# GpSimd adds weight blocks, and a third pair of k tiles takes seven block products for eight, in an encoder's second FFN product

## The chip, the cores and the metric

The kernel runs on one core of a Trainium2 chip. The metric is the device time of one execution in microseconds (us). The engines are TensorE (PE: matmuls; PEld: its weight loads), VectorE (DVE), ScalarE (ACT), GpSimd (POOL) and SyncE (SP, which issues nearly all loads).

## What is computed

Two layers of an encoder over 256 tokens with a width of 2048. Each layer mixes the tokens in three ways (an mLSTM, latent attention, dilated attention), projects the result and ends with a feed-forward part, the stage of this change:

```
h = rms_norm(x, norm_ff)
u = relu(h @ w_ff1)            # 256 x 8192
x = x + (u * u) @ w_ff2        # 8192 -> 2048
```

All is float32. The kernel gets float32 accuracy from a faster matmul type by splitting each operand into a high half (`hi`, rounded) and a low half (`lo`, what the rounding left), so that every block product is three matmuls: hi by hi, hi by lo, lo by hi.

## The kernel before, in words

**Stages.** Each layer runs through the mixers, the output projection, and then four chunks of 2048 of the 8192 FFN columns. A chunk has a first product (16 tiles `u` of 128 columns, 32 weight units) and a second product, in which the 16 tiles are multiplied by their 2048 rows of `w_ff2`. "kp" counts pairs of neighbouring k tiles, 0 to 7.

**The second product.** The output has 2048 columns: four units of 512, taken two at a time (`fast_groups`, line 1272): a left unit g and a right unit g+1, each with two PSUM banks, one for each 128 tokens. A plain step (`token_group`, line 469) takes one weight unit, 128 x 1024 values (two k tiles of 512 columns), and makes 2 k tiles x 2 token tiles x 3 = 12 matmuls of 512 columns. For the kp in `FAST` (line 307), (2, 5), left and right are done together: 2 token tiles x 2 k tiles times 2 k tiles x 2 units is a 2 x 2 product of blocks, and it takes seven block products (21 matmuls) where plain steps take eight (24). For that it needs sums of blocks of both sides. The activations' sums (`act_sums`, line 1253) are made once a chunk. The weights' sums are four adds of 128 x 512 for each such pair, made on DVE, in `Weights.split`, as the first part of a unit of kind "sums". So a pair has four weight units: "first" and "second" (the loaded blocks of the left and the right unit; of the second only half is used), "sums" and "more sums" (two added blocks each). Four more PSUM banks hold products that several sums share; `fast_end` (line 1320) adds them to x, `ff2_end` (line 1368) adds the left and right banks. The order of a group is: left 0, left 1, pair 2, left 3, left 4, pair 5, left 6, left 7, then the six right steps. The last chunk of layer 0 has no pairs.

**Weights.** `Weights` (line 222) walks one list of units for the whole kernel. SP loads a unit into one of three buffers (`wst`); ACT casts it to `hi`; DVE subtracts to get `lo`. Four hi/lo buffers (`B_HL`, line 1397), so units are split up to three ahead of PE. A load is issued for each split unit that was a loaded one. The added blocks lie in `ws`, two tiles of the pool `big` (four tiles), beside the split activation sums `s_hl`.

**Order.** Each engine works through its instructions in program order. That order is written by a planner (`Stream`, line 123): small generators, the tasks, are stepped when their due time has come on a clock that counts the cost of the matmuls, from a table of costs per engine.

**The start.** `warm_up` (line 553) runs `WARM` = 10 products of 128 columns while the first loads are on their way.

The functions that the change touches:

Of the kernel before, what the change touches and what calls it, by code (L numbers as in the profile page):

```python
# [17 lines left out]
P = 128  # L18
# [50 lines left out]
MLA_AT = ((3, 2), (3, 3), (3, 7), (4, 3), (5, 0), (6, 1))  # L69
MARGIN = 0.3  # L70
ML_AT_ONCE = 2
WARM = 10

# [135 lines left out]
def tile2k(c, name, dtype=F32R):  # L209
    return c.t2.tile([P, 512], dtype, tag="t2", name=name)  # L210
# [11 lines left out]
class Weights:  # L222
# [3 lines left out]
    def __init__(self, c, items):  # L226
        self.c, self.items = c, items
        self.srcs = [(i, src, n) for i, (src, n, kind) in enumerate(items) if src is not None]
        self.st, self.hl = {}, {}
        self.i = self.d = self.k = 0  # L230

    def load(self):
        c = self.c
        if self.d == len(self.srcs):
            return
        i, src, n = self.srcs[self.d]
        self.st[i] = c.wp.tile([P, 1024], F32, tag="wst", name="wst", bufs=c.B_ST)
        for cols in self.pieces(i):
            c.nc.sync.dma_start(self.st[i][:, cols], src[:, cols])
        self.d += 1  # L240

    def pieces(self, i):
# [4 lines left out]
    def split(self):  # L247

        c, nc, k = self.c, self.c.nc, self.k
        src, n, kind = self.items[k]  # L250
        hi = c.wp.tile([P, 1024], F32R, tag="whi", name="whi", bufs=c.B_HL)
        lo = c.wp.tile([P, 1024], F32R, tag="wlo", name="wlo", bufs=c.B_HL)
        if kind == "sums":
            a, b = self.st.pop(k - 2), self.st.pop(k - 1)

            x, y = (c.big.tile([P, 1040], F32, tag="big", name="ws") for _ in range(2))
            self.st[k + 1] = y
            pieces, st = [slice(0, 512), slice(512, 1024)], x
        else:
            st = self.st[k] if kind else self.st.pop(k)  # L260
            if kind == "second":
                st = st[:, 512:]
                pieces = [slice(0, 512)]
            elif kind == "more sums":
                st = self.st.pop(k)
                pieces = [slice(0, 512), slice(512, 1024)]
            else:
                pieces = self.pieces(k)

        def parts():  # L270
            if kind == "sums":
# [5 lines left out]
            for cols in pieces:  # L277
                nc.scalar.copy(hi[:, cols], st[:, cols])
            yield
            for cols in pieces:  # L280
                nc.vector.tensor_tensor(out=lo[:, cols], in0=st[:, cols], in1=hi[:, cols].bitcast(F32),
                                        op=ALU.subtract)

        t = c.s.spawn(parts())
        if kind != "more sums":
            c.s.step(t)
        else:
            t.due = max(t.due, self.sums.due)
        if kind == "sums":
            self.sums = t  # L290
        self.hl[k] = (hi, lo, t)
        self.k += 1

    def next(self):
        while self.k < min(len(self.items), self.i + self.c.B_HL - 1):
            loads = self.items[self.k][0] is not None
            self.split()
            if loads:
                self.load()
# [14 lines left out]
def weight_order(c, depth):  # L314
    srcs = []
    for l in range(depth):
# [8 lines left out]
        for ch in range(NCHUNK):  # L325
            srcs += [(c.w_ff1[l, ch * KT + i, half], 1024) for i in range(KT) for half in range(2)]
            if not fast(l, ch, depth):
                srcs += [(c.w_ff2[l, ch, g, kp], 1024) for g in range(NX) for kp in range(KT // 2)]
                continue
            for g in range(0, NX, 2):  # L330
                for kp in range(KT // 2):
                    if kp in FAST:
                        srcs += [(c.w_ff2[l, ch, g, kp], 1024, "first"), (c.w_ff2[l, ch, g + 1, kp], 1024, "second"),
                                 (None, 1024, "sums"), (None, 1024, "more sums")]
                    else:
                        srcs.append((c.w_ff2[l, ch, g, kp], 1024))
                srcs += [(c.w_ff2[l, ch, g + 1, kp], 1024) for kp in range(KT // 2) if kp not in FAST]
    return [(*a, None)[:3] for a in srcs]
# [325 lines left out]
def k_rope(c, z1):  # L664
# [17 lines left out]

    kh = c.cp.tile([P, S], F32R, tag="krh", name="krh", bufs=1)
    kl = c.cp.tile([P, S], F32R, tag="krl", name="krl", bufs=1)
    nc.scalar.activation(kl[MLA_ROPE:], c.const[MLA_ROPE:, :S], AF.Copy, scale=0.0)
# [205 lines left out]
def ml_gates(c, z1):  # L891
# [59 lines left out]

    ahl = c.cp.tile([P, 2, S], F32R, tag="ml_ahl", name="ml_ahl", bufs=1)
    A2 = A.unsqueeze(1).to_broadcast([64, 2, S])
# [170 lines left out]
def mixers(c, prepare, after):  # L1124
    nc, s = c.nc, c.s
    dv = c.cp.tile([P, 2, NT, DIL_H * DIL_DH], F32R, tag="dv", name="dv", bufs=1)
    c.dv = {(i, tt): dv[:, i, tt] for i in range(2) for tt in range(NT)}
# [95 lines left out]
def ffn(c, l, last_layer, depth):  # L1223
# [4 lines left out]
    for ch in range(NCHUNK):  # L1228
        us = [None] * KT
        quick = fast(l, ch, depth)  # L1230
        uf = {kp: tile2k(c, "uf", F32) for kp in FAST} if quick else {}
        sums = {}
        for f in range(KT):
            ps = c.gps.tile([P, 512], F32, tag="g", name="g")
            for half in range(2):
                w_half(c, c.xg, 8 * half, ps, half == 0, half == 1)
            kp, i = divmod(f, 2)
            c.s.spawn(ff1_end(c, ps, f, us, uf[kp][:, i * S:(i + 1) * S] if kp in uf else None))
            if i and kp in uf:
                c.s.spawn(act_sums(c, us, kp, uf[kp], sums))  # L1240
        for g in range(0, NX, 2):
# [10 lines left out]

def act_sums(c, us, kp, u, sums):

# [9 lines left out]
    yield  # L1264
    hl = c.big.tile([P, 1040], F32R, tag="big", name="s_hl")
    nc.scalar.copy(hl[:, :512], sf)
# [5 lines left out]
def fast_groups(c, us, sums, l, ch, g, last, last_layer, nxt):  # L1272
# [11 lines left out]
    left, right = two_banks(c), None  # L1284
    banks = None
    for kp in range(KT // 2):
        if kp not in FAST:
            token_group(c, us, left, 512, [kp])
            continue
        first, end = kp == FAST[0], kp == FAST[-1]  # L1290
        if first:
            right = two_banks(c)
            c.s.until(lambda: c.s.room["m"] >= 4)
            c.s.give(m=-4)
            banks = [new_bank(c, "fast") for _ in range(4)]
        p1, q5, p6, p7 = banks
        c.s.until(lambda: kp in sums)
        s1, s2, s3, s4 = sums[kp]
        w = c.w.next()
        product(p1, u(2 * kp, 0), w, one, first, end)  # L1300
        product(left[0], u(2 * kp + 1, 0), w, two, False, False)
        w = c.w.next()
        product(right[0], s4, w, one, first, False)
        w = c.w.next()
        product(q5, s1, w, one, first, end)
        product(p6, s2, w, two, first, end)
        w = c.w.next()
        product(p7, s3, w, one, first, end)
        product(left[1], u(2 * kp + 1, 1), w, two, False, False)
        if end:  # L1310
            done = c.s.spawn(fast_end(c, banks, g))
    c.s.spawn(ff2_end(c, left, g, l, ch, last_layer, nxt, done))
    kps = [kp for kp in range(KT // 2) if kp not in FAST]
    token_group(c, us, right, 512, kps[:-1] if last else kps, opened=(0,))
    if last:
        last_unit(c, us, right, 512)
    c.s.spawn(ff2_end(c, right, g + 1, l, ch, last_layer, nxt, done))
# [70 lines left out]
def encoder(ctx, tc, xT, x, const, vecs, w_in, w_in1, w_mla, w_out, w_ff1, w_ff2, out):  # L1388
# [30 lines left out]
    c.xts = xts = []  # L1419
    c.mean = c.cp.tile([P, 16], F32, tag="mean", name="mean")[:, :2]  # L1420
    nc.vector.memset(c.mean, 1.0 / D)
# [164 lines left out]
```

## Time and profile before

| | us |
|---|---|
| median of 3 runs | 2108.2 (2107.16 to 2109.35) |
| profiled execution, its own time | 2108.59 |
| its span, first to last instruction | 2106.8 |
| PE busy in the span | 2094.5 |
| DVE busy | 1582.6 |
| ACT busy | 1125.8 |
| POOL busy | 13.8 |

The granted clock of TensorE is 0.999 of full speed over the span. How to read it: busy times are unions over the span, PE's ends are modelled and its matmuls overlap, so the duration shown for one matmul (0.39 us) is longer than the distance to the next. A releaser behind an idle time (`<-`) is what ended it. L104 and L200 are the lines of the helpers that record all DVE, ACT and POOL instructions and all matmuls; so instructions are told apart by their tiles.

### The profile page before, as it was taken

To read this page: it belongs to the slowest core of one execution; us is meant where nothing else is said; L and a number is where in the kernel's file an instruction comes from. 1 tells how busy PE (TensorE), PEld (TensorE's weight loads), DVE (VectorE), ACT (ScalarE), POOL (GpSimd) and SP (SyncE) were. 2 spreads that over 40 slices of the span, in tenths; PEclk is the share of its full clock that TensorE was granted. 3 is DMA by queue.
4 is the path that set the end of the run, shared out by engine and by line. 5 is a ranking of instruction groups with operands and counts; after the bars stand their busy time and mean duration, and the time that the engine had idled before them with its cause. 6 is when DMAs were issued, how large, how long until landed. Compare 5 with 4: busy or idle time off the path is not lost.

```text
span 2106.8 us, 29301 instructions
## 1 busy us (share of the span) xinstructions
PE 2094.5 (99%) x10792; PEld 1791.9 (85%) x10792; DVE 1582.6 (75%) x2624; ACT 1125.8 (53%) x1870; POOL 13.8 (1%) x35
## 2 busy tenths in 40 slices
PE   9999999999999999999999999999999999999999
PEld 8888888888888888888888888888888888888887
DVE  6789865788778778775557888567877787787786
ACT  5777654454455444544456675554544454454453
POOL 1000000000000000001000000000000000000000
PEclk9999999999999999999999999999999999999999
DMA  7544455666656665656555445556665566666665
GB/s 264 162 169 156 150 170 181 194 189 204 191 182 200 200 191 183 210 192 200 181 170 166 140 137 165 175 180 193 190 203 191 178 206 199 189 191 201 190 193 176
DMA packets 109151, 389.91 MB, mean 185 GB/s; under 512 B 12368, under 2 KB 12496, under 8 KB 108752
## 3 DMA queue, kind: packets, MB, share of 16 engines
q1 hardware_dynamic: 107136, 384.71, 57.8%
q10 hardware_dynamic: 1872, 3.33, 0.4%
q8 instruction: 84, 1.38, 0.3%
q14 instruction: 59, 0.48, 0.1%
HBM read 385.90 MB, written 2.10 MB: 184 GB/s over the span
## 4 chain that ended last, share of the span: by engine, by line
PE 95%; DMA 2%; DVE 1%; ACT 1%; issue 0%; ACTq 0%; DVEq 0%
PE g L200 85%; PE fast L200 4%; PE mla_z L200 2%; DMA wst<-w_in 1%; PE oT L200 1%; DVE wlo L104 1%; PE mla_s L200 1%; ACT whi L104 1%; PE ml_h L200 1%; PE pT L206 0%; PE xT L206 0%; PE dil_s L200 0%; DMA wst<-w_ff 0%; PE nkT L206 0%; PE dqkT L206 0%
## 5 line engine op out<-in xcount | busy, mean ns | idle before, releaser
L104 ACT CAST whi<-wst 128x1024 fp32r<-128x1024 f32 (+3 forms) x733 | 749.0, 1025 | 394.5 <-PE g L200 181.8
L104 DVE TENSOR_TENSOR wlo<-wst,whi 128x1024 fp32r<-128x1024 f32 (+3 forms) x733 | 863.6, 1189 | 127.4 <-ACT whi L104 125.5
L200 PE MATMUL g<-whi,u 128*128 128x512 f32 x1712 | 539.9, 390 | 0.0
L200 PE MATMUL g<-xg,whi 128*128 128x512 f32 x2048 | 489.9, 391 | 0.0
L200 PEld LDWEIGHTS g<-xg,whi 128*128 128x128 f32 x2048 | 376.7, 188 | 72.6
L200 PEld LDWEIGHTS g<-whi,u 128*128 128x128 f32 x1712 | 321.6, 188 | 66.7
L200 PE MATMUL g<-whi,xg 128*128 128x512 f32 (+1 forms) x1152 | 371.7, 389 | 1.8 <-ACT whi L104 1.8
L200 PE MATMUL g<-wlo,u 128*128 128x512 f32 x856 | 333.4, 389 | 0.0
L200 PEld LDWEIGHTS g<-xg,wlo 128*128 128x128 f32 x2048 | 262.9, 191 | 11.7 <-ACT xg L104 2.0
L200 PE MATMUL g<-xg,wlo 128*128 128x256 f32 x2048 | 267.4, 283 | 1.1 <-ACT xg L104 1.1
L200 PEld LDWEIGHTS g<-whi,xg 128*128 128x128 f32 x1152 | 215.2, 189 | 39.2 <-ACT whi L104 2.0
L200 PE MATMUL g<-wlo,xg 128*128 128x512 f32 (+1 forms) x576 | 221.0, 384 | 2.4 <-DVE wlo L104 2.4
L104 ACT COPY junk<-g 128x256 f32<-128x256 f32 x128 | 47.8, 373 | 304.9 <-PE g L200 304.9
L200 PEld LDWEIGHTS g<-wlo,u 128*128 128x128 f32 x856 | 160.9, 188 | 33.4
L104 DVE TENSOR_TENSOR junk<-g,junk 128x256 f32<-128x256 f32 x128 | 54.3, 424 | 173.8 <-ACT junk L104 173.8
L200 PE MATMUL g<-whi,y 128*128 128x512 f32 x512 | 164.7, 394 | 0.0
L200 PEld LDWEIGHTS g<-wlo,xg 128*128 128x128 f32 x576 | 109.2, 190 | 20.1 <-DVE wlo L104 3.8
L200 PEld LDWEIGHTS g<-whi,y 128*128 128x128 f32 x512 | 96.2, 188 | 19.4
L200 PE MATMUL g<-wlo,y 128*128 128x512 f32 x256 | 99.8, 390 | 0.0
L104 DVE TENSOR_TENSOR x<-g,x 128x512 f32<-128x512 f32 x80 | 53.4, 688 | 55.6 <-PE g L200 55.6
L104 ACT CAST whi<-ws 128x512 fp32r<-128x512 f32 x112 | 63.8, 619 | 40.5 <-PE g L200 40.5
L104 DVE TENSOR_TENSOR wlo<-ws,whi 128x512 fp32r<-128x512 f32 x112 | 71.7, 687 | 3.7 <-ACT whi L104 1.5
(244 smaller groups left out, 1693.1 us busy)
## 6 DMA issues: line engine op xcount, KB each, us to landing
wst<-w_ff SPq DMA_DIRECT2D x512, 512.0 KB, 4.2
wst<-w_in SPq DMA_DIRECT2D x127, 512.0 KB, 3.6
wst<-w_out SPq DMA_DIRECT2D x64, 512.0 KB, 4.0
wst<-w_in SPq DMA_DIRECT2D x16, 336.0 KB, 3.1
wst<-w_mla SPq DMA_DIRECT2D x12, 416.0 KB, 3.2
x<-x SPq DMA_DIRECT2D x2, 1024.0 KB, 6.0
out<-x ACTq DMA_DIRECT2D x8, 256.0 KB, 2.5
xt<-xT SPq DMA_DIRECT2D x7, 256.0 KB, 6.7
```

Source lines behind the costliest of these rows:

```text
L104: return fn(*args, **kw)
L200: c.nc.tensor.matmul(out, lhsT, rhs, start=start, stop=stop)
```

## The change

- `FAST` is (1, 3, 5): three of eight pairs take seven block products for eight.
- `FAST_ORDER` mixes left (l) and right (r) steps with the pairs (b).
- The two blocks of a pair are loaded into `big` (four tiles, two pairs); the three `wst` buffers hold plain units only. `loads` issues loads in list order as long as there is room.
- The four adds of a pair are POOL instructions, issued right behind its second load. Their results lie in the first half of the second block, in one of two tiles `mix0` and `mix1`, and in a tile of the pool `mla_zs`. The planner takes 5 us for a load (`LANDING`).
- Tiles are shared to make room: the rotary tables lie in `mix0`, three small tiles of the mixers in `mix1`, the split activation sums in `dv`, their unsplit sums in `mla_zs`.
- `WARM` is 14.

```diff
-WARM = 10
+WARM = 14
...
+        if kind:
+            self.st[i] = c.big.tile([P, 1040], F32, tag="big", name="wab")
+        else:
+            self.st[i] = c.wp.tile([P, 1024], F32, tag="wst", name="wst", bufs=c.B_ST)
...
+        if kind == "second":
+            self.sum[i] = t = c.s.spawn(self.add(i))
+            t.last["dma"] = c.s.clk + LANDING
+            c.s.step(t)
+
+    def loads(self):
+
+        while self.d < len(self.srcs):
+            kind = self.srcs[self.d][3]
+            if kind != "second" and (self.out["pair"] == 2 if kind else self.out["plain"] == self.c.B_ST):
+                break
+            self.load()
+
+    def add(self, i):
+
+        c = self.c
+        a, b = self.st[i - 1], self.st[i]
+        self.mix = 1 - getattr(self, "mix", 1)
+        x = c.cp.tile([P, 1024], F32, tag=f"mix{self.mix}", name="ws", bufs=1)
+        y = c.zp.tile([P, 2 * WZ], F32, tag="mla_zs", name="ws")
+        t1, t2, t3, t4 = b[:, :512], x[:, :512], x[:, 512:], y[:, :512]
+        for out, p, q in ((t3, b[:, :512], b[:, 512:1024]), (t1, a[:, :512], b[:, :512]), (t2, t3, a[:, :512]),
+                          (t4, t2, a[:, 512:1024])):
+            c.nc.gpsimd.tensor_tensor(out=out, in0=p, in1=q, op=ALU.add)
+        self.st[i + 1], self.st[i + 2] = (t1, t2), (t3, t4)
...
         def parts():
-            if kind == "sums":
-                t1, t2, t3, t4 = x[:, :512], x[:, 512:1024], y[:, :512], y[:, 512:1024]
-                for out, p, q in ((t3, b[:, :512], b[:, 512:]), (t1, a[:, :512], b[:, :512]), (t2, t3, a[:, :512]),
-                                  (t4, t2, a[:, 512:])):
-                    nc.vector.tensor_tensor(out=out, in0=p, in1=q, op=ALU.add)
-                yield
...
         t = c.s.spawn(parts())
-        if kind != "more sums":
+        if kind and "sums" in kind:
+            t.due = max(t.due, max(self.sum[k - 1 - (kind != "sums")].last.values()))
+        else:
             c.s.step(t)
...
-FAST = (2, 5)
+FAST = (1, 3, 5)
...
+FAST_ORDER = ('l0', 'b1', 'l2', 'r0', 'b3', 'l4', 'r2', 'b5', 'l6', 'l7', 'r4', 'r6', 'r7')
...
-    rope = c.cp.tile([P, 4, NT, MLA_ROPE], F32, tag="rope", name="rope", bufs=1)
-    drope = c.cp.tile([P, 2, NT, 4, DIL_ROT], F32, tag="drope", name="drope", bufs=1)
+    tab = c.cp.tile([P, 1024], F32, tag="mix0", name="rope", bufs=1)
...
+        if quick:
+            hls = c.cp.tile([P, 2 * NT * DIL_H * DIL_DH], F32R, tag="dv", name="s_hl", bufs=1)
...
-    sf = tile2k(c, "sf", F32)
+    sf = c.zp.tile([P, 2 * WZ], F32, tag="mla_zs", name="sf")[:, :512]
```

## Rows read from the trace of the kernel before

**Rows 1.** Page, part 1: busy us (share of the span) x instructions.
```profile
PE 2094.5 (99%) x10792; PEld 1791.9 (85%) x10792; DVE 1582.6 (75%) x2624; ACT 1125.8 (53%) x1870; POOL 13.8 (1%) x35
```
**Rows 2.** Chain of waits, one group: shares; start us, us, what.
```profile
by line: PE g L200 87.2%; PE fast L200 13.4%
...
1515.81 27.91 PE g L200 x123
```
**Rows 3.** Stretches: two neighbouring groups, then a first product.
```profile
core 0: us, PE busy (x) PEld busy (x) DVE busy (x) ACT busy (x) POOL busy (x), PEclk, DMA share, GB/s
1502.00:1544.40 42.40, 42.40 (x188) 34.97 (x187) 35.51 (x45) 20.76 (x27) 0.00 (x0) 1.00 0.64 200
1544.40:1586.70 42.30, 42.30 (x195) 35.21 (x194) 33.58 (x42) 21.00 (x27) 0.00 (x0) 1.00 0.67 211
1586.70:1676.00 89.30, 89.30 (x507) 78.64 (x507) 67.34 (x110) 43.77 (x67) 0.00 (x0) 1.00 0.59 183
```
**Rows 4.** Groups by shape, DVE, first of these stretches: busy us, mean ns | idle before.
```profile
L104 DVE TENSOR_TENSOR wlo<-wst,whi 128x1024 fp32r<-128x1024 f32 x15 | 18.2, 1220 | 4.3 <-ACT whi L104 4.3
L104 DVE TENSOR_TENSOR wlo<-ws,whi 128x512 fp32r<-128x512 f32 x8 | 5.1, 684 | 0.1
L104 DVE TENSOR_TENSOR ws<-ws,wst 128x512 f32<-128x512 f32 x4 | 2.8, 688 | 0.1
L104 DVE TENSOR_TENSOR x<-g,x 128x512 f32<-128x512 f32 x4 | 2.6, 686 | 2.4 <-PE g L200 2.4
...
L104 DVE TENSOR_TENSOR junk<-fast,junk 128x512 f32<-128x512 f32 x3 | 2.1, 684 | 0.0
```
**Rows 5.** Groups by shape, whole span: the copy of a shared bank.
```profile
L104 ACT COPY junk<-fast 128x512 f32<-128x512 f32 x14 | 8.1, 578 | 0.0
```
**Rows 6.** Timeline, POOL and DVE, 992 to 998 us: start us, us.
```profile
992.87 0.46 POOL L104 TENSOR_TENSOR rope<-const,vec 128x128 f32<-128x128 f32 x1 [961.66 <-DMA vec<-vecs]
...
993.81 1.45 DVE L104 TENSOR_TENSOR wlo<-wst,whi 128x1024 fp32r<-128x1024 f32 x1 [0.85 <-ACT whi L104]
...
994.13 1.45 POOL L104 TENSOR_TENSOR rope<-const,vec 128x128 f32<-128x128 f32 x1
...
995.54 0.32 POOL L104 TENSOR_TENSOR drope<-const,vec 128x64 f32<-128x64 f32 x1
...
996.53 1.25 DVE L104 TENSOR_TENSOR wlo<-wst,whi 128x1024 fp32r<-128x1024 f32 x1 [1.27 <-ACT whi L104]
...
996.66 1.31 POOL L104 TENSOR_TENSOR drope<-const,vec 128x64 f32<-128x64 f32 x1
```
**Rows 7.** Page, part 6, DMA issues: count, KB each, median us to landing.
```profile
wst<-w_ff SPq DMA_DIRECT2D x512, 512.0 KB, 4.2
```
**Rows 8.** Timeline, ACT, a pair in the last group: casts of added blocks.
```profile
2064.91 1.14 ACT L104 CAST whi<-ws 128x512 fp32r<-128x512 f32 x2 [1.67 <-PE g L200]
2066.29 1.14 ACT L104 CAST whi<-ws 128x512 fp32r<-128x512 f32 x2 [0.24 <-PE g L200]
```
**Rows 9.** Timeline, the last group: a late load, and PE's wait.
```profile
2075.34 1.05 ACT L104 CAST whi<-wst 128x1024 fp32r<-128x1024 f32 x1 [4.65 <-DMA wst<-w_ff]
...
2078.31 0.50 PE L200 MATMUL fast<-wlo,s_hl 128*128 128x512 f32 x1 [0.84 <-DVE wlo L104]
```
**Rows 10.** Timeline, the start: warm-up products and the first product.
```profile
1.05 4.26 PE L559 MATMUL warm<-ones 128*128 128x128 f32 x20 [1.05 <-DVE mean L104]
...
7.12 0.50 PE L200 MATMUL g<-whi,xg 128*128 128x512 f32 x1 [1.80 <-ACT whi L104]
```
**Rows 11.** Stretches of 1 us at the start, columns as in rows 3.
```profile
8.00:9.00 1.00, 1.00 (x3) 0.78 (x4) 1.00 (x3) 0.98 (x2) 0.00 (x0) 0.60 1.01 397
9.00:10.00 1.00, 1.00 (x4) 0.79 (x3) 0.69 (x2) 1.00 (x3) 0.00 (x0) 0.50 1.01 401
10.00:11.00 1.00, 1.00 (x4) 0.81 (x3) 1.00 (x2) 0.64 (x2) 0.00 (x0) 0.50 1.07 414
11.00:12.00 1.00, 1.00 (x4) 0.77 (x4) 0.77 (x3) 1.00 (x2) 0.00 (x0) 0.70 0.97 389
```

More of the change, by code (lines that the diff above doesn't have):

```diff
@@ L227, in __init__ @@
         self.c, self.items = c, items
-        self.srcs = [(i, src, n) for i, (src, n, kind) in enumerate(items) if src is not None]
-        self.st, self.hl = {}, {}
+        self.srcs = [(i, *item) for i, item in enumerate(items) if item[0] is not None]
+        self.st, self.hl, self.sum = {}, {}, {}
+        self.out = dict(plain=0, pair=0)
         self.i = self.d = self.k = 0
@@ L233, in load @@
         c = self.c
[L234 to L237, printed above, removed]
+        i, src, n, kind = self.srcs[self.d]
+        if kind:
+            self.st[i] = c.big.tile([P, 1040], F32, tag="big", name="wab")
+        else:
+            self.st[i] = c.wp.tile([P, 1024], F32, tag="wst", name="wst", bufs=c.B_ST)
+        self.out["plain"] += not kind
+        self.out["pair"] += kind == "first"
         for cols in self.pieces(i):
@@ L252, in split @@
         lo = c.wp.tile([P, 1024], F32R, tag="wlo", name="wlo", bufs=c.B_HL)
-        if kind == "sums":
[L254 to L258, printed above, removed]
-        else:
[L260 to L268, printed above, removed]
@@ L270, in parts @@
-        def parts():
-            if kind == "sums":
-                t1, t2, t3, t4 = x[:, :512], x[:, 512:1024], y[:, :512], y[:, 512:1024]
-                for out, p, q in ((t3, b[:, :512], b[:, 512:]), (t1, a[:, :512], b[:, :512]), (t2, t3, a[:, :512]),
-                                  (t4, t2, a[:, 512:])):
-                    nc.vector.tensor_tensor(out=out, in0=p, in1=q, op=ALU.add)
-                yield
-            for cols in pieces:
-                nc.scalar.copy(hi[:, cols], st[:, cols])
+        st = self.st.pop(k)
@@ L279, in parts @@
+        if kind and "sums" in kind:
+            pieces = [(slice(i * 512, i * 512 + 512), p) for i, p in enumerate(st)]
+        elif kind == "second":
+            pieces = [(slice(0, 512), st[:, 512:1024])]
+        else:
+            pieces = [(cols, st[:, cols]) for cols in self.pieces(k)]
+        def parts():
+            for cols, p in pieces:
+                nc.scalar.copy(hi[:, cols], p)
             yield
-            for cols in pieces:
-                nc.vector.tensor_tensor(out=lo[:, cols], in0=st[:, cols], in1=hi[:, cols].bitcast(F32),
-                                        op=ALU.subtract)
+            for cols, p in pieces:
+                nc.vector.tensor_tensor(out=lo[:, cols], in0=p, in1=hi[:, cols].bitcast(F32), op=ALU.subtract)
@@ L284, in split @@
         t = c.s.spawn(parts())
-        if kind != "more sums":
+        if kind and "sums" in kind:
+            t.due = max(t.due, max(self.sum[k - 1 - (kind != "sums")].last.values()))
+        else:
             c.s.step(t)
[L287 to L290, printed above, removed]
+        self.out["plain"] -= not kind
+        self.out["pair"] -= kind == "more sums"
         self.hl[k] = (hi, lo, t)
@@ L295, in next @@
         while self.k < min(len(self.items), self.i + self.c.B_HL - 1):
-            loads = self.items[self.k][0] is not None
             self.split()
-            if loads:
-                self.load()
+            self.loads()
         hi, lo, t = self.hl.pop(self.i)
@@ L330, in weight_order @@
             for g in range(0, NX, 2):
-                for kp in range(KT // 2):
-                    if kp in FAST:
+                for at in FAST_ORDER:
+                    kp = int(at[1])
+                    if at[0] == "b":
                         srcs += [(c.w_ff2[l, ch, g, kp], 1024, "first"), (c.w_ff2[l, ch, g + 1, kp], 1024, "second"),
@@ L335, in weight_order @@
                     else:
-                        srcs.append((c.w_ff2[l, ch, g, kp], 1024))
-                srcs += [(c.w_ff2[l, ch, g + 1, kp], 1024) for kp in range(KT // 2) if kp not in FAST]
+                        srcs.append((c.w_ff2[l, ch, g + (at[0] == "r"), kp], 1024))
     return [(*a, None)[:3] for a in srcs]
@@ L950, in ml_gates @@
     yield
[L952 removed]
+    ahl = c.mix[:, 2 * S:].rearrange("p (i s) -> p i s", i=2)
     A2 = A.unsqueeze(1).to_broadcast([64, 2, S])
@@ L1250, in ffn, with act_sums @@
     c.xg = nxt
-def act_sums(c, us, kp, u, sums):
+def act_sums(c, us, kp, u, hls, sums):
     nc = c.nc
@@ L1284, in fast_groups @@
     left, right = two_banks(c), None
-    banks = None
-    for kp in range(KT // 2):
-        if kp not in FAST:
-            token_group(c, us, left, 512, [kp])
[L1289 to L1316, printed above, removed]
+    banks = done = None
+    for n, at in enumerate(FAST_ORDER):
+        kp = int(at[1])
+        more = [b[0] for b in FAST_ORDER[n + 1:]]
+        if at[0] == "b":
+            first, end = kp == FAST[0], kp == FAST[-1]
+            if first:
+                right = two_banks(c)
+                c.s.until(lambda: c.s.room["m"] >= 4)
+                c.s.give(m=-4)
+                banks = [new_bank(c, "fast") for _ in range(4)]
+            p1, q5, p6, p7 = banks
+            c.s.until(lambda: kp in sums)
+            s1, s2, s3, s4 = sums[kp]
+            w = c.w.next()
+            product(p1, u(2 * kp, 0), w, one, first, end)
+            product(left[0], u(2 * kp + 1, 0), w, two, False, False)
+            w = c.w.next()
+            product(right[0], s4, w, one, first, False)
+            w = c.w.next()
+            product(q5, s1, w, one, first, end)
+            product(p6, s2, w, two, first, end)
+            w = c.w.next()
+            product(p7, s3, w, one, first, end)
+            product(left[1], u(2 * kp + 1, 1), w, two, False, False)
+            if end:
+                done = c.s.spawn(fast_end(c, banks, g))
+        elif at[0] == "l":
+            token_group(c, us, left, 512, [kp])
+            if "l" not in more:
+                c.s.spawn(ff2_end(c, left, g, l, ch, last_layer, nxt, done))
+        elif last and not more:
+            last_unit(c, us, right, 512)
+        else:
+            token_group(c, us, right, 512, [kp], opened=(0,))
@@ L1419, in encoder @@
     c.xts = xts = []
-    c.mean = c.cp.tile([P, 16], F32, tag="mean", name="mean")[:, :2]
+    c.mean = c.small.tile([P, 16], F32, tag="mean", name="mean", bufs=1)[:, :2]
     nc.vector.memset(c.mean, 1.0 / D)
```

17 lines of the change are left out of this document (12 added, 5 removed).

## The prediction

> **What bounds the kernel now.** I read the page's busy lines first: TensorE (PE) is busy nearly the whole span, VectorE (DVE) three quarters of it, GpSimd (POOL) hardly at all [rows 1]. A busy PE need not be the bound, so the chain of waits comes next, in one group of the second FFN product (two units of 512 output columns): the shares by line are PE's alone. 123 matmuls take 27.91 us, so a matmul costs 0.227 us [rows 2]. The reader is to see that the stage is paced by the number of matmuls and by nothing else. Then the stretches: two neighbouring groups last 42.4 and 42.3 us, DVE is busy 35.5 and 33.6 us of them, POOL 0 [rows 3]. The count agrees: 12 plain steps of 12 matmuls and two seven-for-eight pairs of 21 are 186 x 0.227 = 42.2 us. Last, DVE's groups of instructions in such a stretch: nearly all of its work there is halves of weights (wlo), the adds of weight blocks (ws) and the ends of the sums (x, junk) [rows 4].
>
> **Matmuls removed.** A pair takes 21 matmuls where two plain steps (left and right of the same kp) take 24. Each group gets one more pair: 3 matmuls, 0.68 us. The ACT copy of a product bank that each group does once counts the groups: 14 [rows 5]. So 42 matmuls x 0.227 = 9.53 us go, all on the path. The loads are the same blocks, so no bytes change.
>
> **DVE's load per group.** From the shapes in [rows 4]: a plain step is one half of 1.22 us; a pair is 1.22 + 0.69 + 4 x 0.69 = 4.65 us, and 4 adds of 0.69 = 2.75 us. The mean of the two stretches is 34.5 us; less two pairs' adds (5.5), less two plain steps (2.4), plus one pair (4.65) leaves 31.3 us in 41.5 us. The activations of the third pair are six small operations per chunk, in the stage of the first product where DVE has 22 us of 89.3 idle [rows 3]: nothing.
>
> **The adds on POOL.** The trace has no 128x512 add there. It has the same kind of instruction at 128 and 64 columns: 0.46 and 0.32 us when left alone [rows 6], that is 2.2 ns a column and 0.18 us fixed, so about 1.3 us for 512 columns (an estimate from these two rows), of which 1.1 us is data. A pair is 5.2 us, three pairs 15.6 us of a 41.5 us group. POOL has room, and the new order loads a pair five or six steps (13 to 16 us) ahead of its use. A load lands 4.2 us after its issue [rows 7]; a pair is two loads behind one more, some 7 us. What is left, 6 to 9 us, covers 5.2 us.
>
> The price is elsewhere. Where a DVE half and a POOL product ran at once, they didn't overlap: the POOL operation of 0.46 us took 1.45 us and ended just after the DVE half, and that half took 1.45 us instead of 1.22; the next meeting looks the same, 1.31 us for 0.32, one operation of each engine in turn [rows 6]. So a 512 column add can hold a DVE half back by up to 1.1 us. Per group the two together want 31.3 + 12 x 1.1 = 44.5 us of 41.5. But the nine operations that take one input from PSUM (four x from g, five x or junk from fast, of which [rows 4] show the commonest: 9 x 0.69 = 6.2 us) are another shape than those that met in the rows; if they run beside an add, 38.3 us do. And of a chunk's six pairs two are added during the first product, where DVE is freer. On the mean it just fits; what counts is lateness at one spot.
>
> That spot is the pair. Four hi/lo buffers stand for the weights, and ACT's casts there wait for PE to give one back [rows 8]. The step after a pair can be cast once the pair's first unit is used: 6 matmuls (1.36 us) after the pair starts, then 1.05 us of cast and 1.22 of lo half make 3.6 us, and PE wants it after 21 matmuls, at 4.8 us, its first lo 0.2 later: 1.3 us spare. One add in between (1.1 us) is covered. In that time DVE also makes the two lo halves of the fourth unit, so up to three adds can get in: 3.3 - 1.3 = 2.0 us lost at most, nothing at least. Two of the three pairs of a group can be hit, by the adds of the pair after them; the third is followed by plain steps and none are loaded then. Per group 0 to 4.0 us; I take 0.25 us, nearest to one add per pair, which is what the spare covers, and a second one now and then: 14 x 0.25 = 3.5 us.
>
> The Trainium skill (SBUF — State Buffer, "Who interferes with whom") says that a VectorE operation with two inputs in SBUF and a GpSimd operation that reads SBUF exclude each other for the whole instruction, and that one with a single SBUF input does not contend. By that rule the first rival below is what the move brings; the trace agrees with its first half (1.45 us for 0.46), and no run here shows the second yet.
>
> **The stall near the end.** Before, PE waited 0.84 us once in this stage, in the last group: a load landed late, so a half was late [rows 9]. The pairs get four buffers of their own and three stay for plain steps, so the loads start earlier: -0.84 us; bounds 0 and -0.84.
>
> **The start.** The 10 warm-up products are 20 records in 4.26 us and end at 5.31; 8 more records take at most 1.70 us and end by 7.01, before the first product at 7.12 [rows 10]: no cost. PE then ran at half clock (1.2 GHz) after its idle 1.8 us, from 8.2 to 11.6 us; the granted shares lose 0.4 + 0.5 + 0.5 + 0.3 = 1.7 us [rows 11]. If the shorter idle keeps the clock up, up to 1.7 us return; but the DMA engines are full there (0.97 to 1.07), so loads may hold PE instead. Between 0 and -1.7 I take -0.5.
>
> **Right units mixed in.** The right sums now end 4.1 us (one step and six matmuls) before the next group opens its right banks; emptying them is 2 x 0.69 us on DVE. Covered; were DVE 2.5 us behind, it would be late. The four product banks have six steps (16 us) to be emptied, against 8 x 0.69 us. SP waits for the adds and halves before it loads a pair into the same buffers, and the loads queued behind wait too; they have three plain steps in hand. Both at nothing. Shared tables (mix, dv) are dead in this stage.
>
> **Sum.** The profiled execution took 2108.6 us (span 2106.8 and 1.8 around it): -9.5 -0.8 -0.5 +3.5 gives 2101.3. The median of the runs shown is 0.4 lower, 2108.2: forecast 2100.9.
>
> **Rivals.**
> 1. Adds and halves take turns in the pairs, and PE waits there: slower. Place: the lo halves of a pair's fourth unit and of the step behind it. Price: 0.8 us at each of two pairs of a group, between the 0 and 2.0 above; 14 x 1.6 = 22.4 us, less 10.8: 2119.8. It decides from 0.77 us per group (10.8 / 14). For it: the one-for-one turns in [rows 6], and 44.5 us wanted of 41.5. Against it: the spare of 1.3 us, and that the adds hit only if a load lands within a couple of microseconds of the pair.
> 2. No lateness at all: 2108.2 - 10.8 = 2097.4. For it: 9 us of DVE free per group, and lookahead of several steps. Against it: the same rows 6.
> 3. Lateness eats the gain, 0.5 to 1.1 us a group: 2104 to 2112.5, say 2108.
>
> **Chances.** Forecast (2098.5 to 2104) 0.35, rival 2 0.15, rival 3 0.15, rival 1 0.35. Faster by over 0.2% (4.2 us, about what a measurement of this kernel can tell from no change) is the forecast and rival 2: 0.50; within it, rival 3: 0.15; slower, rival 1: 0.35. Both signs hold much of it, so the likeliest case's own range is 2098.5 to 2104. The whole range runs from 2095.5 (no lateness and the full clock gain) to 2120 (half of rival 1's cases lie above), which leaves out about 0.2.
>
> **What would show it.** Right: 42 fewer matmuls; POOL adds near 1.3 us alone and 2 to 2.5 us beside a half; lo halves up to a microsecond longer in this stage only; groups of 41.5 to 42 us with PE idle under 0.3 us each; no wait at 2078. Rival 1: PE waits for wlo in every group, at the first or second pair or the step behind, groups of 43 us. Wrong altogether: PE waiting for ACT casts of ws because adds or loads are late, longer groups with DVE half idle, or a change in the mixers' stages.

## The result: slower by 2.5%, with the profile after

The changed kernel takes 2161.3 us (2160.2 to 2161.6, four runs) where the kernel before takes 2107.9 (2107.2 to 2109.4) on the same chip: ratio 1.0254, interval 1.0241 to 1.0267. The forecast was 2100.9, in a range that ended at 2120. The profiled execution took 2161.5 us, its span is 2159.7.

**Where the time went.** Cut by the starts of matmuls, every stage has its old length, to a microsecond, but one: the seven second products with the pairs. They lasted 84.4 to 84.8 us each before, the last one 85.9; now they last 93.7, 92.9, 90.2, 92.2, 90.3, 93.3 and 92.2. The seven differences add up to 51.4 of the 53.5 us. By its count of matmuls such a product should last 366 x 0.227 = 83.1 us, so the matmuls did go, and some 9 us of waits came.

The page's busy lines of after, beside [rows 1]. DVE does 105 us more and POOL 286 us more, although POOL took adds from DVE:

```profile
PE 2105.9 (98%) x10758; PEld 1781.7 (82%) x10758; DVE 1687.5 (78%) x2603; ACT 1155.3 (53%) x1933; POOL 299.7 (14%) x203
```

Stretches of after, beside [rows 3]: a first product, then the two groups behind it (us; busy us and instructions by engine; granted clock; DMA).

```profile
core 0: us, PE busy (x) PEld busy (x) DVE busy (x) ACT busy (x) POOL busy (x), PEclk, DMA share, GB/s
1612.00:1701.00 89.00, 89.00 (x513) 78.64 (x513) 69.30 (x109) 43.50 (x65) 5.41 (x4) 1.00 0.67 213
1701.30:1746.20 44.90, 42.88 (x185) 34.24 (x185) 40.83 (x44) 23.05 (x31) 17.26 (x11) 1.00 0.50 177
1746.20:1791.60 45.40, 42.54 (x183) 33.78 (x183) 41.34 (x41) 23.21 (x29) 17.87 (x10) 1.00 0.43 148
```

The first product is as before. The groups last 45 us where 41.5 were expected, and DVE, which has fewer instructions to do, is busy 41 us of them instead of 31.3. DVE's and POOL's groups by shape over the whole span say why (busy us, mean ns of one), beside [rows 4]:

```profile
L106 DVE TENSOR_TENSOR wlo<-wab,whi 128x1024 fp32r<-128x1024 f32 x42 | 73.8, 1756 | 1.6 <-ACT whi L106 1.6
L106 DVE TENSOR_TENSOR wlo<-wab,whi 128x512 fp32r<-128x512 f32 x84 | 74.9, 910 | 15.0 <-ACT whi L106 15.0
L106 DVE TENSOR_TENSOR wlo<-ws,whi 128x512 fp32r<-128x512 f32 x126 | 118.1, 975 | 20.3 <-ACT whi L106 20.2
L106 DVE TENSOR_TENSOR x<-g,x 128x512 f32<-128x512 f32 x80 | 52.2, 683 | 22.5 <-PE g L202 22.5
L106 POOL TENSOR_TENSOR ws<-ws,wab 128x512 f32<-128x512 f32 x84 | 154.3, 1837 | 3.3
L106 POOL TENSOR_TENSOR wab<-wab 128x512 f32<-128x512 f32 x42 | 66.8, 1591 | 3.3
```

The halves in a pair have grown on the mean, from 1.22 to 1.76 us and from 0.69 to 0.91 and 0.98; the operation with one input in PSUM (x from g) has not (683 ns, 686 before). Taken one by one, the 138 halves that ran beside an add for over 0.1 us took 2.06 and 2.14 us (1024 columns, the pairs' and the plain ones') and 1.42 and 1.50 us (512 columns, of loaded and of added blocks) on the mean; all others of these sizes kept their 1.22 and 0.68. x from g took 676 ns in the 28 cases beside an add, 686 in the other 52. The adds themselves take 1.6 to 1.8 us on the mean. The timeline at three of the four adds of one pair shows one meeting after the other, as in [rows 6] (start us, us):

```profile
1583.97 1.71 POOL L106 TENSOR_TENSOR ws<-wab 128x512 f32<-128x512 f32 x1 [9.07 <-DMA wab<-w_ff]
...
1584.43 1.79 DVE L106 TENSOR_TENSOR wlo<-ws,whi 128x512 fp32r<-128x512 f32 x1
1585.76 1.64 POOL L106 TENSOR_TENSOR wab<-wab 128x512 f32<-128x512 f32 x1
1586.15 2.33 DVE L106 TENSOR_TENSOR wlo<-wst,whi 128x1024 fp32r<-128x1024 f32 x1
1587.36 2.26 POOL L106 TENSOR_TENSOR ws<-ws,wab 128x512 f32<-128x512 f32 x1
```

The reader is to see a strict turn: while both queues are full, the two engines' operations end one after the other, one of each, and each half is longer by one add's data time (1.1 us, the prediction's estimate), 1.79 for 0.69 and 2.33 for 1.22.

**Where PE waits.** The waits of PE's matmuls on wlo in after (us in total, times, longest):

```profile
PE fast L202 <- DVE wlo L106: 22.9, 21, 3.1
PE g L202 <- DVE wlo L106: 21.4, 35, 1.3
```

To get the place, I added up how much later than 0.227 us behind its predecessor each matmul of a group started, by step, as a mean over the seven chunks. A pair has four units here: first (6 matmuls), second (3), sums (6), more sums (6). The first group of a chunk is 3.55 us late: 2.28 in the sums of its first pair, 0.18 in its more sums, 0.53 in the step behind it and 0.62 in the step behind the second pair. The second group is 5.48 late: 2.73 in the first pair's sums and more sums, 1.70 in the step behind it, 0.64 in the one behind the second pair, 0.39 in the plain step and the first unit ahead of these. The third pair and the last five steps are never late. Together 9.03 us a chunk, 63.2 in seven chunks. Before, it was 0.08 and 0.24.

The timeline at the first pair of a second group shows what meets there:

```profile
1742.52 1.29 POOL L106 TENSOR_TENSOR ws<-wab 128x512 f32<-128x512 f32 x1 [16.89 <-DVE wlo L106]
1743.10 1.25 DVE L106 TENSOR_TENSOR x<-x,junk 128x512 f32<-128x512 f32 x1
1743.88 1.64 POOL L106 TENSOR_TENSOR wab<-wab 128x512 f32<-128x512 f32 x1
1744.28 1.28 DVE L106 TENSOR_TENSOR x<-g,x 128x512 f32<-128x512 f32 x2
...
1749.60 1.76 POOL L106 TENSOR_TENSOR ws<-wab 128x512 f32<-128x512 f32 x1
1750.11 5.21 DVE L106 TENSOR_TENSOR wlo<-ws,whi 128x512 fp32r<-128x512 f32 x3
...
1753.04 3.42 POOL L106 TENSOR_TENSOR ws<-ws,wab 128x512 f32<-128x512 f32 x2
...
1753.68 0.50 PE L202 MATMUL fast<-wlo,s_hl 128*128 128x512 f32 x1 [0.75 <-DVE wlo L106]
1755.24 3.44 DVE L106 TENSOR_TENSOR wlo<-wst,whi 128x1024 fp32r<-128x1024 f32 x2
```

The first pair's own adds start only at 1742.5, behind 16.89 us of idling. The row names a half as what ended it, but that half (1741.25 us, of a plain unit) reads and writes nothing that the add uses; the second of the pair's two loads, issued at 1734.7, took 7.7 us to land, and in all 14 groups the first pair's adds start 0.13 to 0.16 us after such a landing. The second pair's four follow at once: POOL adds without a gap from 1742.5 to 1756.5. It is so in all seven second groups: eight adds in a row, from 6 to 8 us ahead of the first pair's start to 7 or 8 us behind it. In first groups the eight, with gaps of up to 1.4 us, run from 7 to 9 us ahead to 3 to 5 us behind it. The third pair's four start 14 to 17 us behind the first pair's start, about when the second pair begins or up to 2.5 us later. Three halves take 5.21 us where three alone take 2.05. In the rows above, x from x and junk, with two inputs in SBUF, takes 1.25 us beside an add (0.69 before), and two x from g take 1.28 us, their old time, beside the next. The chain of waits from 1745 to 1766 us has lost PE its 87% of [rows 2]:

```profile
by line: PE g L202 32.8%; DVE wlo L106 30.1%; issue 21.1%; DVE x L106 9.3%; PE fast L202 7.6%; DVEq L106 0.1%
```

### The profile page after: what moved, and what is told of

Same layout as the page of the kernel before. It is cut to its first block, busy times and chain, and to the rows that moved or that the text cites. A ratio compares the mean times of both kernels' runs of the same rounds, so it can differ in the third digit from the quotient of the medians.

```text
span 2159.7 us, 29541 instructions
## 1 busy us (share of the span) xinstructions
PE 2105.9 (98%) x10758; PEld 1781.7 (82%) x10758; DVE 1687.5 (78%) x2603; ACT 1155.3 (53%) x1933; POOL 299.7 (14%) x203
## 4 chain that ended last, share of the span: by engine, by line
PE 78%; DVE 12%; issue 4%; DMA 3%; ACT 2%; ACTq 0%; SPq 0%; DVEq 0%
PE g L202 70%; DVE wlo L106 8%; DMA wst<-w_in 2%; DVE junk L106 2%; ACT whi L106 2%; PE mla_z L202 2%; PE fast L202 1%; DMA wst<-w_ff 1%; DVE x L106 1%; PE oT L202 1%; PE mla_s L202 1%; PE ml_h L202 0%; PE xT L208 0%; PE pT L208 0%; DVE u L106 0%
## 5 line engine op out<-in xcount | busy, mean ns | idle before, releaser
L106 DVE TENSOR_TENSOR wlo<-wst,whi 128x1024 fp32r<-128x1024 f32 (+2 forms) x649 | 811.1, 1263 | 112.5 <-ACT whi L106 111.3
L106 ACT CAST whi<-wst 128x1024 fp32r<-128x1024 f32 (+2 forms) x649 | 668.2, 1039 | 263.8 <-DMA wst<-w_ff 110.6
L202 PE MATMUL g<-whi,u 128*128 128x512 f32 x1544 | 495.8, 392 | 1.0 <-DVE x L106 1.0
L202 PEld LDWEIGHTS g<-whi,u 128*128 128x128 f32 x1544 | 291.9, 189 | 61.9 <-ACT whi L106 1.4
L202 PE MATMUL g<-wlo,u 128*128 128x512 f32 x772 | 305.5, 396 | 17.7 <-DVE wlo L106 17.6
L106 POOL TENSOR_TENSOR ws<-wab 128x512 f32<-128x512 f32 x42 | 66.5, 1583 | 1669.3 <-DMA wab<-w_ff 1125.5
L106 ACT CAST whi<-wab 128x512 fp32r<-128x512 f32 (+1 forms) x126 | 96.2, 764 | 148.2 <-PE g L202 98.9
L106 DVE TENSOR_TENSOR wlo<-wab,whi 128x512 fp32r<-128x512 f32 (+1 forms) x126 | 146.5, 1192 | 16.6 <-ACT whi L106 16.6
L106 POOL TENSOR_TENSOR ws<-ws,wab 128x512 f32<-128x512 f32 x84 | 154.3, 1837 | 3.3
L106 DVE TENSOR_TENSOR wlo<-ws,whi 128x512 fp32r<-128x512 f32 x126 | 118.1, 975 | 20.3 <-ACT whi L106 20.2
```

Of the source, the lines that this page charges most:

```text
L106: return fn(*args, **kw)
L202: c.nc.tensor.matmul(out, lhsT, rhs, start=start, stop=stop)
```

## Experiments

In the expectations, A is the theory that the adds' reads and the halves' reads take turns and the halves come late at the pair; the other theories put the loss down to something that the adds don't do by reading: the new order with its buffers and loads, the waits for GpSimd's sums, or GpSimd's being slow as such. Diffs are against the changed kernel, unless another is named. A run without a ratio is one execution.

**1. The change without its adds**: the added blocks are left out, and the loaded blocks stand in their places:

```diff
-        for out, p, q in ((t3, b[:, :512], b[:, 512:1024]), (t1, a[:, :512], b[:, :512]), (t2, t3, a[:, :512]),
-                          (t4, t2, a[:, 512:1024])):
-            c.nc.gpsimd.tensor_tensor(out=out, in0=p, in1=q, op=ALU.add)
-        self.st[i + 1], self.st[i + 2] = (t1, t2), (t3, t4)
+        self.st[i + 1], self.st[i + 2] = (b[:, :512], a[:, :512]), (b[:, 512:1024], a[:, 512:1024])
```

> The changed kernel without its 168 GpSimd adds: the sums units are read from the loaded blocks instead, so the added blocks are left out of the computation; loads, order, casts, halves and matmuls stay. Theory A (GpSimd's adds and VectorE's halves shut each other out, and PE waits for the halves): the second products fall from 92 us a chunk to about 83.2 (366 matmuls x 0.227), 128x512 halves are back at 0.69 us, total 2097 to 2100. Theory B (the mixed order, the two-pair load limit or the planner's due times make loads and casts late): second products stay at 88 us or more, total above 2130.

2097.9 us (2096.7 to 2098.1), ratio 0.995 (0.9933 to 0.9967). The second products last 83.0 to 84.5 us. Its stretches of the two groups:

```profile
1662.80:1704.40 41.60, 41.60 (x186) 34.44 (x185) 31.87 (x42) 23.05 (x31) 0.00 (x0) 1.00 0.53 194
1704.40:1745.80 41.40, 41.40 (x184) 34.31 (x183) 31.92 (x40) 23.02 (x29) 0.00 (x0) 1.00 0.50 162
```

Order, buffers, loads and the 42 matmuls together are worth -10 us, near the -10.8 that the prediction's first three terms add up to. The whole loss, 63.4 us, hangs on the adds being there.

**2. The same adds on DVE**, put out by the planner five microseconds after the loads' issue: `c.nc.gpsimd` to `c.nc.vector`, and the splits of the sums wait for them.

> The changed kernel with the four adds of a pair on VectorE (stepped when the load is due, before the casts), all else the same; the whole computation. Theory A: VectorE has 31.3 + 3 x 2.75 = 39.6 us of work in a first group of 41.5 and 34 in the second, and nothing holds its halves back, so little waiting: 2098 to 2106. Theory B: still slow, above 2130. Rival C (VectorE is the bound whichever engine adds): waits at the pairs as now, 2115 to 2130.

2294.7 us, ratio 1.088 (1.0864 to 1.0897): no theory had that. The waits show why, and that it tells nothing of GpSimd:

```profile
DVE ws L106 <- DMA wab<-w_ff: 161.4, 42, 5.6
```

VectorE's queue runs in order. 42 times an add stood at its head, for a block that had not landed, with halves queued behind it. The 84 loads for pairs land 6.0 us after their issue in the changed kernel, by the median, where the planner reckons with 5. GpSimd's queue holds nothing but the adds, so there a late block holds nothing else up.

**3. GpSimd busy, awaited, but only writing**: four fills of the tiles in place of the four adds.

```diff
-        for out, p, q in ((t3, b[:, :512], b[:, 512:1024]), (t1, a[:, :512], b[:, :512]), (t2, t3, a[:, :512]),
-                          (t4, t2, a[:, 512:1024])):
-            c.nc.gpsimd.tensor_tensor(out=out, in0=p, in1=q, op=ALU.add)
+        for _ in range(2):
+            c.nc.gpsimd.memset(x, 1.0)
+            c.nc.gpsimd.memset(y, 1.0)
```

> The changed kernel with each pair's four GpSimd adds replaced by four GpSimd memsets of the tiles of the added blocks (the added values are left out; casts still wait for GpSimd). GpSimd is busy and waited for, but reads nothing. Theory A, and that reading is what shuts out VectorE's two-input operations: no waits, halves at 0.69 and 1.22 us, 2097 to 2101. Rival D (the casts wait for GpSimd's chain as such, or GpSimd slows VectorE whatever it does): second products of 86 to 92 us, total 2120 to 2160.

2098.0 us, as without the adds. Its groups by shape:

```profile
L106 POOL MEMSET ws<- 128x1024 f32 x84 | 80.7, 960 | 900.2 <-DVE junk L106 534.1 <-DVE wlo L106 366.1
L106 POOL MEMSET ws<- 128x896 f32 x84 | 71.3, 849 | 828.7 <-DVE s_hl L106 828.7
L106 DVE TENSOR_TENSOR wlo<-ws,whi 128x512 fp32r<-128x512 f32 x126 | 82.8, 687 | 44.7 <-ACT whi L106 44.7
L106 DVE TENSOR_TENSOR wlo<-wab,whi 128x1024 fp32r<-128x1024 f32 x42 | 51.1, 1217 | 1.6 <-ACT whi L106 1.6
```

POOL works 152 us. The fills wait for their tiles and not for loads, so they stand earlier than the adds and no cast is held up by them, but 146 halves still ran beside one for over 0.1 us, and they kept their old 0.69 and 1.22 us. So GpSimd's being busy costs nothing, and its adds, which read SBUF, cost 63 us. A GpSimd operation that reads one tile only was not tried.

In the changed kernel ACT's casts did wait for the added blocks, 7.6 us in eight waits, all in second groups. In the run with one tile for the sums (experiment 8) they wait 7.0 us, also eight times, and PE is late by only 0.08 us a chunk at the sums of the second groups' first pairs; so these waits alone do not make the loss.

The Trainium skill (SBUF — State Buffer, "Who interferes with whom") says that a VectorE instruction with two inputs in SBUF contends with a GpSimd instruction that reads SBUF, and not with one that only writes it. The trace agrees: the halves beside these fills took 0.69 and 1.22 us. The Trainium skill says there too that a VectorE instruction with at most one input in SBUF, outside the two-port performance modes, does not contend with GpSimd. The trace of the changed kernel agrees: x from g took 676 ns beside an add.

**4. The old order with the adds on GpSimd**, the only edit against the kernel before:

```diff
-                    nc.vector.tensor_tensor(out=out, in0=p, in1=q, op=ALU.add)
+                    nc.gpsimd.tensor_tensor(out=out, in0=p, in1=q, op=ALU.add)
```

> The kernel before with one edit: the adds of its two pairs per group go to GpSimd (old order, old buffers, WARM 10). Theory A: 8 adds a group, each holding a half back by up to 1.1 us; the changed kernel lost 4.5 us a group to 12 adds, so some 3 us x 14 = 42, total 2140 to 2155. Theory B (the new order and buffers are at fault): within 5 us of the kernel before, 2103 to 2113.

2167.0 us, above what A expected, and far from what the order would need to be the cause. Two pairs a group and no new buffers, and the second products still last 92.4 to 94.0 us. The adds are put out with the split of the sums there, directly ahead of them, and PE is latest in the sums of second groups: 1.50 us a chunk at the first pair and 4.15 at the second. So this run's loss is not of turns alone: ACT's casts wait 19.4 us (30 times) for added blocks, and TensorE's granted clock was 0.50 (1.2 GHz) in six stretches of its second products, 30.7 us in all, which at half speed is some 15 us (an estimate from these stretches). The halves beside the adds:

```profile
L104 DVE TENSOR_TENSOR wlo<-ws,whi 128x512 fp32r<-128x512 f32 x112 | 93.8, 889 | 2.0 <-ACT whi L104 1.2
L104 DVE TENSOR_TENSOR wlo<-wst,whi 128x512 fp32r<-128x512 f32 x30 | 51.0, 1702 | 0.1
```

**5. The adds on DVE when the second unit is split**, so behind its load:

```diff
-            c.nc.gpsimd.tensor_tensor(out=out, in0=p, in1=q, op=ALU.add)
+            c.nc.vector.tensor_tensor(out=out, in0=p, in1=q, op=ALU.add)
...
+        if kind == "second":
+            self.sum[k] = c.s.spawn(self.add(k))
+            c.s.step(self.sum[k])
```

> The changed kernel with a pair's adds on VectorE, issued when its second unit is split (all of the computation), not at its load: in e2 VectorE stood 161 us in front of adds whose load had not landed, and all halves behind them stood too. Theory A (GpSimd's reads were the whole loss): VectorE has 39.6 us of work in 41.5, the load landed long before; 2098 to 2106. Rival C (with three pairs VectorE is the bound whichever engine adds): waits of 1 us or more at the pairs, 2115 to 2130.

2107.4 us (2104.7 to 2109.5), ratio 0.9995 (0.9985 to 1.0004), just above A's range. VectorE with 12 adds of 0.69 us more per group is 54 us better than GpSimd doing them. What is left is 1.7 us of lateness in second groups, 1.18 of it in the second unit of the first pair, where the four adds stand ahead of that unit's half.

**6 to 8. One add or two on GpSimd (6, 7), and all four later (8).** With one add (t3) or two (t3, t2) the other sums are read from loaded blocks:

```diff
+        t3 = x[:, 512:]
+        for out, p, q in ((t3, b[:, :512], b[:, 512:1024]),):
...
+        self.st[i + 1], self.st[i + 2] = (b[:, :512], a[:, :512]), (t3, a[:, 512:1024])
```

> The changed kernel with one GpSimd add per pair, not four (the other three added blocks are left out; loaded blocks stand in for them). The prediction held that the spare of 1.3 us covers one add: then under 0.3 us lost per group, 2098 to 2102. If loss goes with the number of adds: a quarter of 64 us, about 2114.

> The same with two GpSimd adds per pair (the other two added blocks are left out). If a spare covers the first add: between 2102 and 2115. If loss goes with the number of adds: half of 64 us, about 2130.

One add: 2098.0 us, nothing lost. Two: 2112.9. Four, as in the change: 2161.3. Over the 2097.9 without adds that is 0, 15 and 63 us for 42, 84 and 168 adds. So the loss is no price per add; it fits a spare that is used up first, as far as one execution of each can tell. With one add the halves are longer as well (0.75 and 0.82 us for 0.69), and DVE does 33.3 and 33.8 us in the groups instead of 31.9, but PE, except for 1 us in the first chunk, waits no more than without adds:

```profile
L106 DVE TENSOR_TENSOR wlo<-wab,whi 128x512 fp32r<-128x512 f32 x168 | 121.3, 745 | 34.8 <-ACT whi L106 34.8
...
L106 DVE TENSOR_TENSOR wlo<-ws,whi 128x512 fp32r<-128x512 f32 x42 | 34.5, 821 | 43.6 <-ACT whi L106 43.6
```

The place was tried by itself, with all four adds on GpSimd: one tile for the sums instead of two, so that a pair's adds wait until the halves of the pair before are done.

```diff
-        self.mix = 1 - getattr(self, "mix", 1)
+        self.mix = 0
```

> The changed kernel with one tile mix0 for all pairs in place of two in turn: a pair's adds can't start before the casts and halves of the pair before it are done, so they run beside plain steps and not in the pair before. Theory A with the place named in the prediction (the halves of a pair and of the step behind it): the waits at those spots shrink, second products of 84 to 88 us, total 2105 to 2135. If the place doesn't matter (the sum of VectorE's and GpSimd's time is the bound): 90 us or more, 2150 to 2175.

2118.4 us: 43 of the 63 us are back, though GpSimd reads as much as before and the adds got longer. The sums' halves are free of them now, and the plain halves and those of the pair's first two units have them:

```profile
L106 DVE TENSOR_TENSOR wlo<-ws,whi 128x512 fp32r<-128x512 f32 x126 | 80.0, 681 | 0.8 <-ACT whi L106 0.7
L106 DVE TENSOR_TENSOR wlo<-wab,whi 128x1024 fp32r<-128x1024 f32 x42 | 90.2, 2148 | 1.6 <-ACT whi L106 1.6
```

PE waits in the steps behind the pairs instead, 1.2 us in first groups and 1.4 of 1.9 us in second ones. So most of the loss was the adds of the next pair over the sums of this one.

**9 to 12. Versions meant to be faster**: the adds when the sums are split, one on GpSimd and three on DVE, or all four on DVE; then both again with the first pair one plain step later.

```diff
+            if kind == "sums":
+                for out, p, q in self.rest.pop(k):
+                    nc.vector.tensor_tensor(out=out, in0=p, in1=q, op=ALU.add)
+                yield
...
-FAST_ORDER = ('l0', 'b1', 'l2', 'r0', 'b3', 'l4', 'r2', 'b5', 'l6', 'l7', 'r4', 'r6', 'r7')
+FAST_ORDER = ('l0', 'l2', 'b1', 'l4', 'r0', 'b3', 'r2', 'l6', 'b5', 'l7', 'r4', 'r6', 'r7')
```

> The changed kernel (all of the computation) with one add of a pair on GpSimd at its load, the one that reads the second block alone, and the other three on VectorE, issued when the sums unit is split, behind the casts of the pair's first two units. One GpSimd add per pair cost nothing (e8), and VectorE has 31.3 + 3 x 2.06 = 37.5 us of 41.5. Theory A: 2097 to 2101, faster than the kernel before. If VectorE's adds or the shut-outs still make halves late: 2104 to 2112.

> The same with all four adds on VectorE when the sums unit is split (39.6 us of 41.5). In e5 PE's wait stood at the second unit of the second group's first pair (1.2 us), whose half lay behind the adds; here the adds come after it. Theory A: 2098 to 2104, the added 0.69 us per pair eating part of the spare. If VectorE is simply full: 2106 to 2115.

Both missed: 2119.9 (ratio 1.0059, 1.0045 to 1.0072) and 2121.2 (1.0062, 1.0049 to 1.0074). The halves are undisturbed in the second (685 ns), yet PE waits 1.9 and 1.3 us per group, nearly all in the sums of the first pair: the adds stand just ahead of these halves in VectorE's queue, behind the ends of the stage or group before. In the first group at 1677 us they start 0.8 us ahead of the pair.

> e10 with another order of steps: two plain steps ahead of a group's first pair, as in the kernel before, and two between pairs (l0 l2 b1 l4 r0 b3 r2 l6 b5 l7 r4 r6 r7). In e10 PE waited in one place alone, 1.3 and 1.8 us at the sums unit of the first pair of a group, which comes one plain step after the ends of the group before. Theory A: with one more step ahead of it the wait goes, 2097 to 2101. If the wait moves to another pair (VectorE full): 2106 to 2120.

> e11 (all four adds on VectorE at the sums unit) with the same order. Theory A: the wait of 1.9 and 1.3 us at the first pair goes, 2098 to 2103; a difference to e12 is the price of the fourth add on VectorE. If VectorE is full at 39.6 of 41.5 us: 2106 to 2118.

With the pair one step later: 2108.4 us with one add on GpSimd (1.0003, 0.9994 to 1.0012), which misses A (its 1.3 us of lateness in second groups is 0.85 in their first plain step and 0.50 in the first pair's sums), and 2099.8 with none (2098.6 to 2100.9, ratio 0.9961, 0.9949 to 0.9974, kernel before 2107.6). The last, as A had it, is the one that beats both kernels; in its first group at 1666 us the adds start 2.9 us ahead of the pair. Its groups, where the 12 adds are DVE's:

```profile
1665.70:1707.40 41.70, 41.70 (x185) 34.44 (x185) 38.79 (x53) 22.84 (x31) 0.00 (x0) 1.00 0.54 185
1707.40:1748.90 41.50, 41.50 (x184) 34.07 (x183) 39.50 (x53) 22.28 (x29) 0.00 (x0) 1.00 0.55 179
```

VectorE is busy 39 us of 41.6 and PE is busy throughout. In the version that moves one add of four to GpSimd, adds and halves of DVE grow:

```profile
L106 DVE TENSOR_TENSOR ws<-ws,wab 128x512 f32<-128x512 f32 x84 | 66.2, 789 | 1.5
...
L106 DVE TENSOR_TENSOR wab<-wab 128x512 f32<-128x512 f32 x42 | 36.4, 867 | 0.0
```

It takes 28.7 us of adds off DVE (42 x 683 ns) and gives back 8.4 + 7.3 + 2.8 us on the adds and the 512-column halves of wab alone (688, 692 and 687 ns each in the version with none). Other operations with two SBUF inputs grow too, and in all DVE is busy 1662.8 us with the add moved away and 1652.7 us with it; the version with the add moved is 8.6 us slower.

## Why the prediction was wrong

Its sum had -9.5, -0.8, -0.5 and +3.5. The last term failed: lateness at the pairs, from the adds' reads and the halves' taking turns.

**The adds' price, 0.25 us per group, was 4.5** (63.2 us over 14 groups). The mechanism and the sign are rival 1's, which had the same chance as the forecast; its place (the fourth unit and the step behind) holds 5.5 of the 9.0 us a chunk, and the third unit, the sums, which it did not name, 3.1. Rival 1 priced it at 1.6, and the bound given for it was 4.0 at most. Three things were sized wrong in that one step:
- It counted only the step behind a pair, with the two halves of the fourth unit in the way and a spare of 1.3 us. The largest term of a first group is 2.28 us in the sums themselves: what VectorE does ahead of them, the last operations of the first product included, grows by up to 1.1 us each time, and that adds up along VectorE's queue while PE needs six and three matmuls for the first two units. In the group whose first pair starts at 1704.07 us (alone these take 0.43, 0.43, 0.69 and 2.05 us):

```profile
1702.72 1.07 DVE L106 SCALAR_TENSOR_TENSOR junk<-junk 128x256 f32<-128x256 f32 x1
1703.82 1.42 DVE L106 TENSOR_TENSOR junk<-junk,r_row 128x256 f32<-128x256 f32 x1
1705.17 1.78 DVE L106 TENSOR_TENSOR wlo<-wab,whi 128x512 fp32r<-128x512 f32 x1
1706.88 2.98 DVE L106 TENSOR_TENSOR wlo<-ws,whi 128x512 fp32r<-128x512 f32 x3
```

- It let up to three adds in. In second groups eight follow without a gap: the first pair's load lands 6 to 8 us ahead of the pair, as the prediction had it ("What is left, 6 to 9 us, covers 5.2 us"), but beside VectorE's operations the four adds take 6.5 to 8.0 us and not 5.2, and by then the second pair's blocks have landed too. That "the adds hit only if a load lands within a couple of microseconds of the pair" was no argument against it: a queue of four or eight adds lasts 6 to 14 us.
- It priced two of three pairs alike. The first takes most, with its own and the second's adds around it: 6.6 to 9.5 us instead of 4.8. The second, with the third's, costs 0.6 us in the step behind it, and the third, as said there, nothing.

The mean per group, "44.5 us wanted of 41.5", came out near: DVE does 41 us, 9 more than without adds. Over the span it is 142 us for 168 adds, 0.85 each and not 1.1; operations with a PSUM input ran beside them undisturbed, as supposed. It was right that the mean nearly fits and that lateness at one spot counts. The mistake was to price the spot by what the spare covers. (Two ends in the prediction are added up wrong, and nothing hangs on them: 2108.2 - 9.5 - 0.8 - 1.7 is 2096.2 and not 2095.5, and 1.1 us a group leads to 2112.8 and not 2112.5.)

**What held.** The matmuls: the change without adds gains 10.0 us, where 9.5 had been worked out for them. DVE's 31.3 us per group: 31.9. The add alone: 1.30 to 1.31 us (four first adds that met no two-input operation), where 1.3 had been worked out from [rows 6]. The spare that covers one add per pair: one add per pair costs nothing (experiment 6). Right units and shared tables: no stage outside the second products changed by more than 1 us.

**What didn't come.** The -0.84 us near the end: even without adds the last second product takes 84.5 us, where the others take 83.0 to 83.3, by three small delays at the last group's first pair and the step behind it (0.3, 0.4 and 0.2 us) and some shorter ones. Why there was not tried. And the start's -0.5 us. The clock stayed up, as hoped, but PE then waits for a half at 11.65 us that goes back to a load, for which its cast waited until 9.28:

```profile
11.00:12.00 1.00, 0.35 (x2) 0.31 (x3) 1.00 (x3) 0.93 (x2) 0.00 (x0) 1.00 0.96 379
```

Beside [rows 11] the granted clock is 1.00 and PE's busy share falls to 0.35, with the DMA engines as full as before. The first output projection starts at 260.5 us in the changed kernel, at 259.6 before, and at 258.9 in two versions, one with 14 warm-up products (without adds) and one with 10 (old order): the warm-up decides nothing that these runs can tell.

## What to carry to other kernels

Before an operation with SBUF inputs goes to an idle GpSimd, count what operations with two SBUF inputs VectorE has queued in the same microseconds: 0.69 us taken from VectorE cost it up to 1.1 us here, at the place where it was already last. By the busy time of whole runs, the 168 adds cost VectorE 142 us when GpSimd did them (1687.5 against 1545.4 without adds) and 107 us when VectorE did them itself (1652.7 in the best version). The idle engine's share of the span says nothing against that; a row where both ran at once does, and its price is to be multiplied along the whole queue, not at one step. And an add on VectorE is nearly free where VectorE's queue has room ahead of its reader: the best version, with all 168 on VectorE and the first pair one plain step later, is 1.9 us above the version without adds (whose order is the changed kernel's).

## Not expected of the hardware

- Lateness costs twice. In the first second product PE idles, and then the granted clock falls to 0.50 (1.2 GHz), for 3.4 us, three times in all inside these products (columns as in [rows 3]):

```profile
454.00:455.00 1.00, 0.00 (x0) 0.00 (x0) 1.00 (x2) 0.92 (x2) 1.00 (x1) 1.00 0.00 0
455.00:456.00 1.00, 0.23 (x1) 0.23 (x2) 1.00 (x2) 1.00 (x2) 0.17 (x1) 1.00 0.00 0
456.00:457.00 1.00, 1.00 (x5) 0.77 (x5) 1.00 (x3) 0.38 (x1) 0.00 (x0) 0.79 0.00 0
457.00:458.00 1.00, 1.00 (x4) 0.80 (x3) 1.00 (x3) 0.37 (x1) 0.00 (x0) 0.50 0.00 0
```

- Other work on DVE pays too: two of its 128x256 operations with both inputs in SBUF rose from 425 ns to 488 and 583 on the mean, the one of the same size with a PSUM input stayed at 424.
- A GpSimd fill of 128x1024 took 0.96 us beside VectorE's halves without any effect on them, where an add of half the columns held them back by 1.1 us.
